# Rescaled tokens from the third group on, and five more pieces by Strassen's scheme, in a two-layer encoder trunk

## Chip, cores and metric

The kernel runs on one core of one Trainium2 chip. Five engines work from their own instruction queues and wait for one another by semaphores: TensorE (PE; its weight loads are listed as PEld), VectorE (DVE), ScalarE (ACT), GpSimd (POOL) and SyncE (SP), which issues the transfers. The metric is the device time of one execution in microseconds, as a median of several runs. The profile comes from one execution.

## What is computed

Two layers over x of shape (1, 512, 1024). Each layer has a token mixer, a cross-attention and an output projection, and then a gated feed-forward part, where the change lies:

```python
def rms_norm(x, g):
    y = xf * lax.rsqrt(jnp.mean(xf * xf, axis=-1, keepdims=True) + EPS)
    return y * g

def conv_ffn(h, w_up, conv_w, conv_b, w_down):
    u = h @ w_up                                   # 1024 -> 2 x 2816
    c = causal depthwise convolution of width 3 of u, + conv_b
    a, g = jnp.split(c, 2, axis=-1)
    return (jax.nn.silu(g) * a) @ w_down           # 2816 -> 1024
...
    h = rms_norm(x, ffn_norm[i])
    x = x + conv_ffn(h, w_up[i], conv_w[i], conv_b[i], w_down[i])
```

The row scale rsqrt(...) is one number per token, the same for all channels. The gain g is one number per channel.

## The kernel before

Activations lie transposed: 128 channels on the partitions, 512 tokens in the free dimension. `xT[k]` (k = 0 to 7) are the eight residual tiles of a layer. Every operand of a matmul is kept as a high and a low part in fp32r (names ending in h or hi, and l or lo); a product is three matmuls, hi x hi, hi x lo and lo x hi (`product`, L401 to L409). Splits are a cast on ScalarE and a subtraction on VectorE: `split_weights` and `combined` for weights (L257, L260, L308, L309, L311, L312), `split` for tokens (L365, L366), `parts_of` for everything else (L1278, L1279).

The feed-forward part (`ffn`) runs over eleven groups q = 0 to 10, in parts of four, four and three (`HALVES`). A group has 256 channels of a (piece `ua`) and 256 of g (piece `ug`). A plain piece is two products, n = 0 and 1, each of eight contraction tiles, 48 matmuls of 128x512 in all. In the text a group's products with the same n, one of a and one of g, are called a step; steps are counted by 2 * q + n. After each product comes `conv`: a multiply by the row scale `rB` on VectorE, in place in PSUM (L1248), then the first tap on ScalarE (L1250) and two taps on VectorE (L1251, L1252). Silu of g is on ScalarE (L1455), the product a * g on VectorE (L1457), and its split (L1278, L1279). The tokens that TensorE reads, `xh` and `xl`, hold x times the gain without the row scale: they are made before `rB` exists. `rB` is computed in `row_scales` behind the first step of group 0.

Pieces listed in `SEVEN` go through `up_by_seven`: Strassen's scheme in Winograd's form, seven products of halves in place of eight. It has 12 matmuls of 128x512 for the first pair of contraction tiles and 63 of 128x256 (L1233) for the other three pairs. It takes four PSUM banks rather than two, sums of weight blocks (`block_sums`, GpSimd, L285), sums of tokens for three pairs (`token_sums`, once per layer) and a decoding of the banks (L1238 to L1244: one copy on ScalarE, six additions on VectorE). `token_sums` scales two tiles by the gain on ScalarE (`scaled`, L1321), combines them by four operations of GpSimd (`combine`, L1286) and splits the results; `SUMS_AT` says behind which step this is done for which pair. The middle sums of a * g for the down projection (`mid_sums`) go through the same `combine`.

After each part comes a down projection (`down`, L1358 for its Strassen products; its decoding and the residual additions are L1375 to L1382). PSUM banks are taken in turn by the eight entries of `TURNS`: mm, mm, sm, sm, lg, lg, tp, tp. Weights come by transfers of 512 KB into three raw buffers, and are split as their six split buffers (`WB`) come free, in program order. The order of the instructions on each engine is settled when the kernel is built: the scheduler interleaves the code above by its dependences; `keep_in_program_order` holds some GpSimd work to the order of the code.

## Time and profile before

| | us |
|---|---|
| median of 3 runs | 1144.44 (1144.1 to 1144.5) |
| profiled execution | 1144.21 |
| its span in the trace | 1142.4 |
| TensorE busy, weight loads busy | 1137.8, 992.9 |
| VectorE, ScalarE, GpSimd busy | 934.7, 619.8, 279.5 |
| groups 0 to 3 of layer 0, first down projection | 241.0 to 328.5, 328.5 to 368.8 |
| groups 4 to 7, second down projection | 368.8 to 454.7, 454.7 to 495.1 |
| groups 8 to 10 | 495.1 to 558.6 |

A row of a timeline reads: start, duration, engine, line, operation, output<-inputs, shapes, and in brackets the idle time before it with what ended it. A row of groups reads: line, engine, operation, names, shapes, count, then busy time and mean ns of one, then the idle time before it and its releasers. Engines pipeline, so the distance from one start to the next is often shorter than the duration: a matmul of 128x512 is listed with 0.39 us and the next starts 0.23 us later.

### The profile page before, as it was taken

Reading aid. Unit: us, or ns where it says so; the run is one execution under the profiler, and the core shown is the slowest. Engines: PE = TensorE matmul, PEld = TensorE weight load, DVE = VectorE, ACT = ScalarE, POOL = GpSimd, SP = SyncE. Lnnn points to the kernel's source line nnn. Section 1 sums busy time; section 2 is a strip of 40 time slices with the busy share of each in tenths; the row PEclk is TensorE's granted clock in tenths of the full one; section 3 lists DMA queues with packets and bytes.
Section 4 is the critical chain, followed back from the end, with each engine's and each line's share of the span. In section 5 each row is a group of like instructions: output and inputs, shape, how many; then the busy total and the mean of one; then the engine's idle time right before and its main releaser. Section 6 shows DMA issues by size and latency. Waiting matters only on the chain.

```text
span 1142.4 us, 17519 instructions
## 1 busy us (share of the span) xinstructions
PE 1137.8 (100%) x6554; PEld 992.9 (87%) x6554; DVE 934.7 (82%) x1553; ACT 619.8 (54%) x1097; POOL 279.5 (24%) x326
## 2 busy tenths in 40 slices
PE   9999999999999999999999999999999999999998
PEld 7888888888899888999888888988888989899888
DVE  7676778689989899999777636778888988999997
ACT  6676687556554355445557634536664434544552
POOL 0000000004364425760000000000246432575240
PEclk9999999999999999999999999999999999999999
DMA  8522242132313332243252330234222243234312
GB/s 290 175 74 96 79 143 70 59 112 78 125 57 129 100 104 74 89 134 112 88 178 72 94 96 19 82 125 140 74 74 93 93 129 93 92 94 130 105 52 102
DMA packets 39666, 117.87 MB, mean 103 GB/s; under 512 B 4767, under 2 KB 7256, under 8 KB 39582
## 3 DMA queue, kind: packets, MB, share of 16 engines
q1 hardware_dynamic: 39150, 116.37, 32.1%
q8 instruction: 51, 0.84, 0.3%
q10 hardware_dynamic: 432, 0.39, 0.1%
q14 instruction: 33, 0.27, 0.1%
HBM read 112.54 MB, written 4.21 MB: 102 GB/s over the span
## 4 chain that ended last, share of the span: by engine, by line
PE 99%; DMA 0%; DVE 0%; issue 0%; SPq 0%; ACT 0%
PE ps_mm L407 6%; PE ps_mm L408 6%; PE ps_mm L409 6%; PE ps_mm L385 6%; PE ps_mm L387 6%; PE ps_mm L386 6%; PE ps_lg L1358 5%; PE ps_sm L407 4%; PE ps_sm L408 4%; PE ps_sm L409 4%; PE ps_mm L1358 4%; PE ps_tp L1358 4%; PE ps_sm L1358 3%; PE ps_tp L224 3%; PE ps_lg L1233 3%; PE ps_tp L408 3%
## 5 line engine op out<-in xcount | busy, mean ns | idle before, releaser
L260 DVE TENSOR_TENSOR wlo<-raw,whi 128x1024 fp32r<-128x1024 f32 (+5 forms) x165 | 185.9, 1139 | 76.4 <-ACT whi L257 74.2
L257 ACT CAST whi<-raw 128x1024 fp32r<-128x1024 f32 (+5 forms) x165 | 157.2, 967 | 101.2 <-PE ps_mm L408 20.3
L285 POOL TENSOR_TENSOR wsum<-raw 128x256 f32<-128x256 f32 (+1 forms) x112 | 99.6, 910 | 115.2 <-DMA raw<-in_wpack_dram 56.5
L385 PE MATMUL ps_mm<-whi,xsh 128*128 128x512 f32 (+2 forms) x328 | 126.4, 385 | 0.0
L387 PE MATMUL ps_mm<-whi,xsl 128*128 128x512 f32 (+2 forms) x328 | 123.1, 375 | 0.0
L386 PE MATMUL ps_mm<-wlo,xsh 128*128 128x512 f32 (+2 forms) x328 | 122.9, 375 | 0.0
L407 PE MATMUL ps_mm<-xsh,whi 128*128 128x512 f32 x294 | 115.6, 393 | 0.0
L408 PE MATMUL ps_mm<-xsl,whi 128*128 128x512 f32 x294 | 114.7, 390 | 0.0
L409 PE MATMUL ps_mm<-xsh,wlo 128*128 128x512 f32 x294 | 114.6, 390 | 0.0
L311 ACT CAST whi<-wsum 128x1024 fp32r<-128x1024 f32 (+1 forms) x56 | 53.6, 957 | 49.3 <-POOL wsum L285 43.7
L1286 POOL TENSOR_TENSOR cvo<-cvo 128x256 f32<-128x256 f32 x56 | 47.4, 866 | 134.3 <-DVE cvo L1457 133.2
L408 PE MATMUL ps_sm<-xsl,whi 128*128 128x512 f32 x202 | 78.7, 389 | 0.0
L407 PE MATMUL ps_sm<-xsh,whi 128*128 128x512 f32 x202 | 78.7, 389 | 0.0
L409 PE MATMUL ps_sm<-xsh,wlo 128*128 128x512 f32 x202 | 78.6, 389 | 0.0
L312 DVE TENSOR_TENSOR wlo<-wsum,whi 128x1024 fp32r<-128x1024 f32 (+1 forms) x56 | 67.1, 1198 | 7.1 <-ACT whi L311 5.6
L385 PEld LDWEIGHTS ps_mm<-whi,xsh 128*128 128x128 f32 x328 | 61.8, 188 | 11.4 <-issue 1.0
L387 PEld LDWEIGHTS ps_mm<-whi,xsl 128*128 128x128 f32 x328 | 61.7, 188 | 11.3
L386 PEld LDWEIGHTS ps_mm<-wlo,xsh 128*128 128x128 f32 x328 | 61.9, 189 | 10.1
L1263 POOL MEMSET xsh<- 128x128 f32 x2 | 0.4, 210 | 276.4 <-PE ps_sm L408 189.9
L409 PEld LDWEIGHTS ps_mm<-xsh,wlo 128*128 128x128 f32 x294 | 55.2, 188 | 11.6
L407 PEld LDWEIGHTS ps_mm<-xsh,whi 128*128 128x128 f32 x294 | 55.3, 188 | 11.3 <-issue 0.3
L408 PEld LDWEIGHTS ps_mm<-xsl,whi 128*128 128x128 f32 x294 | 55.3, 188 | 11.2 <-DVE xsl L366 0.4
(446 smaller groups left out, 3173.7 us busy)
## 6 DMA issues: line engine op xcount, KB each, us to landing
raw<-in_wpack_dram SPq DMA_DIRECT2D x178, 512.0 KB, 3.6
xt<-in_x_t_dram SPq DMA_DIRECT2D x15, 256.0 KB, 5.1
raw<-in_wpack_dram SPq DMA_DIRECT2D x15, 256.0 KB, 2.9
raw<-in_wpack_dram SPq DMA_DIRECT2D x8, 384.0 KB, 3.3
xres<-xt SPq DMA_DIRECT2D x8, 256.0 KB, 3.4
xt<-xres SPq DMA_DIRECT2D x8, 256.0 KB, 5.5
out_dram<-xt SPq DMA_DIRECT2D x7, 256.0 KB, 2.0
bt<-bias_d SPq DMA_DIRECT2D x6, 256.0 KB, 4.0
```

Source lines behind the costliest of these rows:

```text
L257: ins = A.copy(hi[:, c], raw[:, c])
L260: V.tensor_sub(lo[:, c], raw[:, c], hi[:, c].bitcast(F32))
L285: tc.keep_in_program_order(getattr(G, "tensor_" + op)(o, x, y))
L311: A.copy(h1[:, m], wsum[:, m])
L312: V.tensor_sub(l1[:, m], wsum[:, m], h1[:, m].bitcast(F32))
L385: mm(p, sh[k][:, blk(b)], hi, start=k == 0, stop=False)
L386: mm(p, sh[k][:, blk(b)], lo, start=False, stop=False)
L387: mm(p, sl[k][:, blk(b)], hi, start=False, stop=k == KT - 1)
L407: mm(p, hi[:, blk(n)], bh, start=i == first, stop=False)
L408: mm(p, hi[:, blk(n)], bl, start=False, stop=False)
L409: mm(p, lo[:, blk(n)], bh, start=False, stop=i == last)
L1358: mm(banks[c][b][:, h], w, v, start=b not in seen[c], stop=m == nq - 1 and t == 2 and i in close)
```

## The change

From group 2 on the tokens already carry the row scale: `rescale` multiplies `xT[k]` by `rB` on GpSimd, splits the result with the gain, and collects the eight tiles in `fresh`; `FRESH_AT` says behind which step which tiles are made (three behind step 0, three behind step 1, two behind step 2). `conv` leaves the multiply out where the tokens are `fresh`. The token sums are now made of scaled tokens (`scaled` multiplies by gain and `rB` in one instruction of VectorE, before by the gain alone on ScalarE) and stand behind steps 4, 5 and 6 rather than 1, 2 and 3. Their tiles and those of `fresh` swap the buffers that they come from. Five pieces are added to `SEVEN`: `ua` of group 4 and `ug` of group 5 in both layers, `ua` of group 10 in layer 0. In group 5 both pieces then go by Strassen's scheme, one behind the other, and hold all eight banks; before, group 9 of layer 0 alone did so.

```diff
-SEVEN = (('ua', 0, 5), ('ua', 0, 6), ('ua', 0, 8), ('ua', 0, 9), ('ua', 1, 5), ('ua', 1, 6), ('ua', 1, 8), ('ua', 1, 9), ('ug', 0, 9))
-SUMS_AT = {1:(4,5),2:(0,1),3:(2,3)}
+SEVEN = (('ua', 0, 4), ('ua', 0, 5), ('ua', 0, 6), ('ua', 0, 8), ('ua', 0, 9), ('ua', 1, 4), ('ua', 1, 5), ('ua', 1, 6), ('ua', 1, 8), ('ua', 1, 9), ('ug', 0, 5), ('ug', 1, 5), ('ug', 0, 9), ('ua', 0, 10))
+SUMS_AT = {4: (4, 5), 5: (0, 1), 6: (2, 3)}
+FRESH_AT = {0: (0, 1, 2), 1: (3, 4, 5), 2: (6, 7)}
...
+        fresh = []
+
+        def rescale(ks):
+            for k in ks:
+                t = ctile()
+                tc.keep_in_program_order(G.tensor_mul(t, xT[k], rB))
+                hi, lo = split_tiles(pool, "vs", 12) if k < 6 else split_tiles()
+                split(hi, lo, t, c_ffn(l, k))
+                fresh.append((hi, lo))
+
         def conv(p, j):
-            V.tensor_mul(p, p, rB)
+            if tokens is not fresh:
+                V.tensor_mul(p, p, rB)
...
         def scaled(k):
             t = ctile()
-            A.activation(t, xT[k], AF.Copy, scale=c_ffn(l, k))
+            V.scalar_tensor_tensor(t, xT[k], c_ffn(l, k), rB, op0=ALU.mult, op1=ALU.mult)
             return t
...
-            tiles = [split_tiles(pool, "vs", 12) for _ in range(2)]
+            tiles = [split_tiles() for _ in range(2)]
...
+                if q == 2:
+                    tokens = fresh
...
+                    if 2 * q + n in FRESH_AT:
+                        rescale(FRESH_AT[2 * q + n])
                     if 2 * q + n in SUMS_AT:
                         token_sums(SUMS_AT[2 * q + n])
```

GpSimd's queue in the feed-forward part of layer 0, from the first entry behind `row_scales` on. Of before, a token sum (the rows with wsum), the middle sums of group 0, then the next token sums:

```order
L1286 TENSOR_TENSOR wsum<-cvo 128x256
L1286 TENSOR_TENSOR wsum<-cvo,wsum 128x256
L1286 TENSOR_TENSOR wsum<-cvo 128x256
L1286 TENSOR_TENSOR wsum<-cvo,wsum 128x256
L1286 TENSOR_TENSOR cvo<-cvo 128x256 x4
```

Of the change (L1253 is `rescale`, L1298 `combine`, L286 the sums of a weight block):

```order
L1253 TENSOR_TENSOR cvo<-xt,rB 128x512 x6
L1298 TENSOR_TENSOR cvo<-cvo 128x256 x4
L1253 TENSOR_TENSOR cvo<-xt,rB 128x512 x2
L1298 TENSOR_TENSOR cvo<-cvo 128x256 x4
L1298 TENSOR_TENSOR wsum<-cvo 128x256
L1298 TENSOR_TENSOR wsum<-cvo,wsum 128x256
```

The eight multiplies stand around group 0's middle sums, and the first token sum has moved behind group 1's.

VectorE's queue in group 2, from the first product of its step 4 on. Of before:

```order
L1248 TENSOR_TENSOR ps_mm<-ps_mm,rB 128x512
L1457 TENSOR_TENSOR cvo<-cvo 128x512
L1279 TENSOR_TENSOR vsl<-wsum,vsh 128x512
L1279 TENSOR_TENSOR mid<-cvo,mid 128x256
L1251 SCALAR_TENSOR_TENSOR cvo<-ps_mm,cv_81,cvo 128x511
L1252 SCALAR_TENSOR_TENSOR cvo<-ps_mm,cv_81,cvo 128x510
```

Of the change (L1263 and L1264 are the taps of `conv`, L1333 is `scaled`):

```order
L1263 SCALAR_TENSOR_TENSOR cvo<-ps_mm,cv_81,cvo 128x511
L1264 SCALAR_TENSOR_TENSOR cvo<-ps_mm,cv_81,cvo 128x510
L1333 SCALAR_TENSOR_TENSOR cvo<-xt,cols,rB 128x512
L1263 SCALAR_TENSOR_TENSOR cvo<-ps_mm,cv_81,cvo 128x511
L1333 SCALAR_TENSOR_TENSOR cvo<-xt,cols,rB 128x512
L1264 SCALAR_TENSOR_TENSOR cvo<-ps_mm,cv_81,cvo 128x510
L1291 TENSOR_TENSOR mid_3061<-cvo,mid_3060 128x512 x2
```

The multiplies by `rB` are gone, and the scalings of the token sums stand between the taps.

TensorE's queue in group 5 of layer 0, where its g piece starts. Of before (plain, behind the last matmuls of the a piece):

```order
L1233 MATMUL ps_lg<-vsl,whi 128x256
L1233 MATMUL ps_lg<-vsh,wlo 128x256
L407 MATMUL ps_mm<-xsh,whi 128x512
L408 MATMUL ps_mm<-xsl,whi 128x512
L409 MATMUL ps_mm<-xsh,wlo 128x512
```

Of the change, in the same piece, where its first pair of tiles ends and the 256-column products begin:

```order
L408 MATMUL ps_sm<-xsh,whi 128x512
L409 MATMUL ps_sm<-xsl,whi 128x512
L410 MATMUL ps_sm<-xsh,wlo 128x512
L1234 MATMUL ps_sm<-vsh,whi 128x256
L1234 MATMUL ps_sm<-vsl,whi 128x256
L1234 MATMUL ps_sm<-vsh,wlo 128x256
```

The piece has changed from 48 wide matmuls into two banks to 12 wide and 63 narrow ones into four.

## The prediction

> **What bounds the kernel now.** First the page: its busy line, the granted clock, the chain's shares by engine.
>
> ```profile
> span 1142.4 us, 17519 instructions
> PE 1137.8 (100%) x6554; PEld 992.9 (87%) x6554; DVE 934.7 (82%) x1553; ACT 619.8 (54%) x1097; POOL 279.5 (24%) x326
> PEclk9999999999999999999999999999999999999999
> PE 99%; DMA 0%; DVE 0%; issue 0%; SPq 0%; ACT 0%
> ```
>
> TensorE is busy from end to end at full clock, and the chain that ends last is TensorE for 99%. A busy PE could still hide gaps, so next come its waits (for whom; us in total, times, longest).
>
> ```profile
> PE ps_tp L512 <- PEq L1524: 0.8, 1, 0.8
> PE ps_mm L586 <- DVE wlo L260: 0.3, 1, 0.3
> PE ps_mm L586 <- ACT xsh L365: 0.2, 1, 0.2
> ```
>
> All waits are 1.3 us, none in the feed-forward part. So the time is the length of TensorE's own instruction stream; another engine costs something only when it becomes late for TensorE. Removing work from VectorE (82% busy) is worth nothing by itself.
>
> Third, windows cut at the first matmul of each piece: plain, Strassen (sixth group's a), plain behind it (its g), and the ninth group's pair, both Strassen. The window's length is the piece's time.
>
> ```profile
> core 0: us, PE busy (x) PEld busy (x) DVE busy (x) ACT busy (x) POOL busy (x), PEclk, DMA share, GB/s
> 379.74:390.62 10.88, 10.88 (x49) 9.02 (x48) 9.37 (x12) 5.58 (x8) 2.43 (x4) 1.00 0.18 49
> 390.62:400.90 10.28, 10.28 (x77) 9.81 (x75) 7.57 (x9) 4.78 (x8) 5.14 (x6) 1.00 0.49 152
> 400.90:411.80 10.90, 10.90 (x50) 9.02 (x49) 9.14 (x14) 5.06 (x8) 2.79 (x4) 1.00 0.15 51
> 516.26:526.54 10.28, 10.28 (x77) 9.81 (x75) 8.85 (x13) 6.12 (x10) 0.00 (x0) 1.00 0.36 104
> 526.54:536.84 10.30, 10.30 (x78) 9.81 (x77) 10.22 (x15) 5.66 (x8) 0.00 (x0) 1.00 0.36 129
> ```
>
> **The change, part by part. First the five pieces.** By the code a plain piece has 48 matmuls of 512 columns: 10.88 / 48 = 0.227 us each. A Strassen piece has 12 of 512 and 63 of 256: (10.28 - 12 x 0.227) / 63 = 0.120 us each. So 36 of 512 go (8.16 us) and 63 of 256 come (7.56): 0.60 us saved; about 0.02 is given back where a plain piece follows (10.90 for 10.88). The side-by-side pair, here 10.28 and 10.30, behaves like two single ones. Five pieces at 0.58 us: **-2.9 us**, bounds 2.8 and 3.0. The order of TensorE's instructions has 135 = 5 x 27 rows more, so all five are really converted; SyncE's has as many as before, so no transfers are added.
>
> The Trainium skill has a rule that speaks against this sum. Its page "TensorE: Matmul & The Clock Gate", section "Back-to-back issue gap", gives a sustained spacing of about 131 ns at 512 columns and 81 ns at 128; a straight line between them would put 256 columns at 98 ns (estimate). By that the pieces would lose 63 x 0.098 - 36 x 0.131 = 1.5 us each, 7.3 us in all. The trace does not agree: 0.227 and 0.120 us, measured on this kernel's operands.
>
> **The row scale.** From the third group on the product is already scaled, so VectorE's multiply by rB (L1248), four per group in nine groups a layer, goes: 36 x 0.69 = 24.8 us. VectorE gains per layer eight low halves of the rescaled tokens (like L366) and six scalings that ScalarE had (L1321): 14 x 0.75 = 10.5 us. Each new piece adds six decoding adds and more weight splits.
>
> ```profile
> L1248 DVE TENSOR_TENSOR ps_sm<-ps_sm,rB 128x512 f32<-128x512 f32 x28 | 19.3, 691 | 1.7 <-PE ps_sm L409 1.7
> L366 DVE SCALAR_TENSOR_TENSOR xsl<-xt,cols,xsh 128x512 fp32r<-128x512 f32 x16 | 12.0, 747 | 0.8 <-ACT xsh L365 0.8
> L1239 DVE TENSOR_TENSOR cvo<-cvo,ps_tp 128x256 f32<-128x256 f32 x4 | 1.7, 421 | 2.1 <-ACT cvo L1238 2.1
> L260 DVE TENSOR_TENSOR wlo<-raw,whi 128x1024 fp32r<-128x1024 f32 x125 | 153.0, 1237 | 67.3 <-ACT whi L257 65.4 <-PE ps_lg L790 1.3
> L260 DVE TENSOR_TENSOR wlo<-raw,whi 128x896 fp32r<-128x896 f32 x9 | 11.4, 1265 | 1.7 <-ACT whi L257 1.5
> L312 DVE TENSOR_TENSOR wlo<-wsum,whi 128x512 fp32r<-128x512 f32 x12 | 10.7, 890 | 3.1 <-PE ps_lg L1233 1.6 <-ACT whi L311 1.5
> L309 DVE TENSOR_TENSOR wlo<-raw,whi 128x768 fp32r<-128x768 f32 x44 | 49.7, 1130 | 0.6 <-ACT whi L308 0.6
> L312 DVE TENSOR_TENSOR wlo<-wsum,whi 128x1024 fp32r<-128x1024 f32 x44 | 56.4, 1282 | 4.0 <-ACT whi L311 4.0
> ```
>
> A new piece: decoding 4 x 0.42 + 2 x 0.69 = 3.1 us, splits 1.27 + 0.89 + 1.13 + 1.28 = 4.57 in place of 2 x 1.24, so +2.1: together 5.2 us of VectorE. Over a whole layer VectorE gets lighter, by 24.8 - 10.5 less two or three times 5.2. That is no gain in time, since nobody waits for it; it only pays for the pieces: in the sixth group, side by side, 16.7 busy us of the two windows above - 4 x 0.69 + 5.2 = 19.1 of 20.6, so it fits. GpSimd makes eight weight sums more per piece, some 7 us at 0.9, and has 5.14 + 2.79 there. All of this costs 0 while both stay ahead.
>
> It does not get lighter at once. Groups three and four also inherit the token sums (six low halves) that stood three pieces earlier.
>
> ```profile
> 285.00:328.52 43.52, 43.52 (x193) 36.06 (x192) 39.81 (x49) 22.87 (x34) 21.00 (x25) 1.00 0.29 93
> ```
>
> Of the 39.8 us, 8 x 0.69 = 5.5 go; 6 x 0.75 = 4.5 (scalings), about 2.5 more token-sum halves at 0.96 = 2.4 (row below) and one token half of 0.75 come: 42.0 of 43.5 us, 1.5 to spare where it had 3.7. I take this as no delay: part of the old 3.7 was waiting, between the rB multiply and the ScalarE step that needed it, and this hop is gone there. Below nothing it can't bring time either, as TensorE has no wait there.
>
> ```profile
> L1279 DVE TENSOR_TENSOR vsl<-wsum,vsh 128x512 fp32r<-128x512 f32 x12 | 11.5, 962 | 4.2 <-ACT vsh L1278 4.2
> L1286 POOL TENSOR_TENSOR cvo<-cvo 128x256 f32<-128x256 f32 x56 | 47.4, 866 | 134.3 <-DVE cvo L1457 133.2
> L285 POOL TENSOR_TENSOR wsum<-raw,wsum 128x256 f32<-128x256 f32 x44 | 49.5, 1124 | 3.5
> ```
>
> **GpSimd's eight multiplies** of 128x512 have no row. The nearest are 256-column ones: 0.87 us (the same cost, if a start-up dominates) up to 2 x 1.12 = 2.25; I take 1.8, twice 0.9, since its duration follows width in the nearest rows. Six come before the first mid sums, two behind them, queued on GpSimd where the token sums were. They cost nothing if the tokens are ready when the third group starts. The last one is the test.
>
> ```profile
> 284.55 0.39 PE L408 MATMUL ps_tp<-xsl,whi 128*128 128x512 f32 x1
> 289.99 0.39 PE L408 MATMUL ps_mm<-xsl,whi 128*128 128x512 f32 x1
> L257 ACT CAST whi<-raw 128x1024 fp32r<-128x1024 f32 x125 | 129.5, 1051 | 76.4 <-DMA raw<-in_wpack_dram 17.4 <-PE ps_mm L408 12.4 <-PE ps_sm L408 12.0
> L365 ACT ACTIVATE xsh<-xt,cols 128x512 fp32r<-128x512 f32 x16 | 11.5, 717 | 3.9 <-DVE xt L1131 3.9
> 273.88 3.41 POOL L1286 TENSOR_TENSOR cvo<-cvo 128x256 f32<-128x256 f32 x4 [1.99 <-DVE cvo L1457]
> ```
>
> GpSimd: mid sums until 277.3, then two multiplies, 281. On ScalarE the eighth token's cast stands behind a weight cast that waits for the second-last matmul at 284.55, done about 284.8: 284.8 + 1.05 + 0.72 = 286.6, its low half on VectorE 287.3. TensorE needs it at 289.99: 2.7 us to spare. Behind that cast on ScalarE stand the second group's last convolution step and silu, whose banks nobody needs before the fourth group. GpSimd itself has 4 us before it enters that chain.
>
> **Sum:** 1144.21 - 2.9 = 1141.3 for the profiled execution (span 1142.4 - 2.9 = 1139.5, and the 1.8 us around it). The median of before lies 0.23 higher, so the median after is **1141.5 us**. What a measurement of this kernel can tell from no change is about 0.2%, 2.3 us; the forecast lies only 0.6 beyond it.
>
> **Rivals. (1) VectorE late in the first down projection.** This one ends slower. TensorE's tightest place is there, in both layers:
>
> ```profile
> 356.75 1.21 DVE L312 TENSOR_TENSOR wlo<-wsum,whi 128x1024 fp32r<-128x1024 f32 x1
> 359.36 0.28 PE L1358 MATMUL ps_lg<-mid,wlo 128*128 128x256 f32 x1
> 905.76 1.21 DVE L312 TENSOR_TENSOR wlo<-wsum,whi 128x1024 fp32r<-128x1024 f32 x1
> 908.24 0.28 PE L1358 MATMUL ps_lg<-mid,wlo 128*128 128x256 f32 x1
> ```
>
> The low weights end 1.40 us (359.36 - 357.96) and 1.27 us before their matmul. If VectorE comes d later out of the fourth group, TensorE loses (d - 1.40) + (d - 1.27). It is faster than the bound only for d under 1.6 and slower than before by the bound for d over 3.9. What could make d: 42.0 - 39.8 = 2.2 us if none of the idle time is used, and a slower VectorE beside GpSimd:
>
> ```profile
> 284.88 1.22 DVE L1279 TENSOR_TENSOR vsl<-wsum,vsh 128x512 fp32r<-128x512 f32 x1
> 287.16 0.68 DVE L1279 TENSOR_TENSOR vsl<-wsum,vsh 128x512 fp32r<-128x512 f32 x1
> 284.37 1.18 POOL L1286 TENSOR_TENSOR wsum<-cvo,wsum 128x256 f32<-128x256 f32 x1
> ```
>
> The same operation takes 1.22 beside a running GpSimd sum and 0.68 without. By the order of GpSimd two token sums more, eight operations at 0.87, fall into these 43.5 us: 7 us, 16% of the time. About half of VectorE's 49 instructions there read two tiles of SBUF; 0.16 x 25 x 0.54 = 2.2. Together d = 4.4: 2 x 4.4 - 2.67 = 6.1 us lost, **1147.6**. With half of it, d = 2.2, 1.7 are lost: 1143.2. For it: the tight 42.0. Against it: the idle time that goes with the hop.
>
> The same point is a rule of the Trainium skill: "GPSIMD Engine Reference", section "Key points", says GpSimd shares its SBUF interfaces with VectorE and contends with VectorE's instructions that have two SBUF inputs. It speaks against the change, which gives both engines more of just these; by it rival 1, without it the forecast. The trace agrees: 1.22 beside 0.68 us.
>
> **(2) The rescaled tokens come late.** The weight cast ahead of the eighth token needs its transfer, whose buffer is freed by a split behind the mid sums' halves.
>
> ```profile
> raw<-in_wpack_dram SPq DMA_DIRECT2D x178, 512.0 KB, 3.6
> ```
>
> Mid sums done at 277.3, their casts and halves and that split about 280.2, landed 283.8: before the matmul that the cast waits for. With the four sums at 1.8 each (7.1 for 3.41) it lands at 287.5, and 1.05 + 0.72 + 0.75 later, 290.0, the token is ready: 0 to 0.3 us a layer. From there each microsecond counts once per layer: 1 us gives 1141.5 + 2 x 1.2 = **1143.9**.
>
> **(3) Side by side fills all eight banks.** The seventh group's first piece needs banks that the sixth's decoding and convolution must have left.
>
> ```profile
> 534.18 0.74 DVE L1252 SCALAR_TENSOR_TENSOR cvo<-ps_sm,cv,cvo 128x510 f32<-128x510 f32 x1
> 536.84 0.40 PE L407 MATMUL ps_sm<-xsh,whi 128*128 128x512 f32 x1
> ```
>
> In the ninth group this is met with 1.9 us (536.84 - 534.92). The new places are lighter (no rB multiply, 1.4 us a pair), but have GpSimd's sums ahead of the weights. Late by 2 us in each layer: 4 less the 1.9 already free, 1143.6 at most; I expect 0.
>
> **(4) It doesn't do what it says**: weight loads pace the narrow matmuls. In a Strassen window the loads take 9.81 / 75 = 0.131 us each; at that pace a piece has 63 x 0.131 + 12 x 0.227 = 11.0 us, 0.1 over the plain one: 1144.44 + 0.5 = **1144.9**. The windows show the loads overlapped, 10.28 us for the piece, so this would have to come only with the new places. By the Trainium skill's spacing quoted above the change would even end at 1144.44 + 7.3 = 1151.7; the rows speak against it, and its chance is inside this rival's.
>
> **Chances.** Forecast 0.57; rival 1 0.25 (half of it within the bound, half slower); rival 2 0.07 and rival 3 0.07, both mostly within; rival 4 0.04. So faster by over 0.2% 0.57, within 0.26, slower 0.17. The range goes from 3.0 saved and the half microsecond of waits that could go, 1141.0, to **1147.0**, which takes in rivals 2 to 4 and the larger part of rival 1; its last part above that is under 0.15.
>
> **What would show it.** Right: TensorE's windows of the fifth group's and sixth group's first and second pieces at 10.28 to 10.30 in both layers, the eleventh's first piece too, TensorE's waits at 1.3 us, and a span near 1139.5. Wrong by rival 1: a wait of ps_lg, ps_mm or ps_tp at the down projection's matmuls (L1358 before) for wlo; by rival 2, a wait of ps_mm for xsl where the third group starts; by rival 3, a wait for VectorE's last convolution step. If a wait shows where I have none of these, a weight or token sum of GpSimd is late, and the chain there will name it.

## The result, and the profile after

The changed kernel takes **1156.55 us** (median of four runs, 1156.29 to 1157.15) against 1144.43 (four runs, 1144.1 to 1144.5): 1.0107 times as long, with an interval of 1.009 to 1.0125, or 12.1 us slower. The forecast was 1141.5 with a range up to 1147.0; the time lies far outside. The profiled execution took 1157.15 us, its span is 13.0 longer than before. Groups are counted from one below, as in the prediction: the sixth is group 5 of the code.

The page's head, with the chain's shares by engine:

```profile
span 1155.4 us, 17931 instructions
PE 1141.2 (99%) x6689; PEld 999.7 (87%) x6689; DVE 942.3 (82%) x1549; ACT 625.9 (54%) x1116; POOL 353.4 (31%) x382
PE 75%; DVE 17%; POOL 3%; issue 2%; ACT 2%; DMA 1%; DVEq 0%; ACTq 0%; POOLq 0%
```

VectorE's share of the span is what it was, 82%, and TensorE still reads 99% (100% before). Only the chain tells that something has turned: it was TensorE for 99%, and now runs for a quarter through VectorE, GpSimd and what they are issued. TensorE's waits in the feed-forward parts name the places:

```profile
PE ps_lg L1370 <- ACT whi L312: 3.3, 2, 1.8
PE ps_lg L1370 <- DVE wlo L313: 2.5, 4, 0.9
PE ps_sm L408 <- DVE cvo L1264: 2.2, 2, 1.1
PE ps_sm L1370 <- DVE mid L1291: 1.3, 2, 1.1
PE ps_tp L408 <- DVE cvo L1264: 0.6, 2, 0.4
PE ps_mm L409 <- DVE xsl L367: 0.3, 1, 0.3
```

L1370 is the down projection's narrow matmul (L1358 before), L408 a wide one of the up projections. A wait is counted from the modelled end of the matmul ahead, so the distance from start to start grows by up to 0.28 us more. That distance gives the whole account (us, from TensorE's first matmul of a stretch to that of the next):

| stretch | before | after | difference |
|---|---|---|---|
| layer 0, third and fourth groups | 43.52 | 44.33 | +0.81 |
| layer 0, first down projection | 40.32 | 46.03 | +5.71 |
| layer 0, fifth to eighth groups | 85.90 | 86.49 | +0.59 |
| layer 0, ninth to eleventh groups | 63.56 | 62.99 | -0.57 |
| layer 1, first down projection | 40.32 | 45.83 | +5.51 |
| layer 1, fifth to eighth groups | 85.90 | 86.66 | +0.76 |

They add to 12.81; what stands ahead of the third group is 0.23 later, and all other stretches are as long as before, within 0.05 in all. So the table accounts for the 13.0 us between the spans. The pieces and the stretches of layer 0 as windows of after; the first two rows are the third and fourth groups and the first down projection, then the fifth group's a, the sixth's a and g, the seventh's a and the eleventh's a:

```profile
core 0: us, PE busy (x) PEld busy (x) DVE busy (x) ACT busy (x) POOL busy (x), PEclk, DMA share, GB/s
285.23:329.56 44.33, 44.05 (x193) 35.88 (x192) 41.70 (x50) 21.32 (x32) 26.57 (x27) 1.00 0.28 84
329.56:375.59 46.03, 42.83 (x337) 42.01 (x336) 43.03 (x55) 21.64 (x31) 33.14 (x34) 0.96 0.26 83
375.59:385.89 10.30, 10.30 (x77) 9.81 (x76) 8.65 (x13) 3.60 (x6) 4.99 (x5) 1.00 0.58 177
396.80:407.07 10.27, 10.27 (x76) 9.80 (x75) 8.18 (x12) 5.73 (x10) 2.65 (x3) 1.00 0.19 53
407.07:417.73 10.66, 10.46 (x78) 9.80 (x76) 8.70 (x13) 4.32 (x7) 7.85 (x10) 1.00 0.30 98
417.73:429.33 11.60, 10.51 (x76) 9.86 (x76) 11.38 (x17) 6.67 (x10) 0.00 (x0) 1.00 0.48 138
544.17:554.47 10.30, 10.30 (x78) 9.81 (x76) 10.06 (x15) 6.70 (x11) 0.00 (x0) 1.00 0.41 136
```

The converted pieces are as short as forecast: 10.30 for the fifth and eleventh groups' a, and 10.66 for the sixth's g, of which 0.36 is a wait at its end. So five pieces did bring their 2.9 us. In the fifth to eighth groups they hide part of the loss: 0.59 and 0.76 are two pieces (-1.16) and 1.75 and 1.92 lost at waits. By far the largest part, 11.2 us, was lost in the two first down projections.

What happens there is read best from GpSimd's own row of work. Before, the sums of the down projection's first and second weight block start one behind the other (the first two rows; a block's sums are L285 before and L286 after). The third row is the next block:

```profile
318.69 1.44 POOL L285 TENSOR_TENSOR wsum<-raw 128x256 f32<-128x256 f32 x2
321.60 2.36 POOL L285 TENSOR_TENSOR wsum<-raw 128x256 f32<-128x256 f32 x2
328.87 2.16 POOL L285 TENSOR_TENSOR wsum<-raw 128x256 f32<-128x256 f32 x2 [2.36 <-DVE wlo L312]
```

After, the four sums of the third token sum (L1298) stand between them:

```profile
322.53 1.88 POOL L286 TENSOR_TENSOR wsum<-raw 128x256 f32<-128x256 f32 x2
...
326.67 0.74 POOL L1298 TENSOR_TENSOR wsum<-cvo 128x256 f32<-128x256 f32 x1
...
329.86 1.18 POOL L1298 TENSOR_TENSOR wsum<-cvo,wsum 128x256 f32<-128x256 f32 x1
333.67 2.38 POOL L286 TENSOR_TENSOR wsum<-raw 128x256 f32<-128x256 f32 x2 [2.63 <-DVE wlo L313]
```

The second block starts 12.1 us later than before. GpSimd works for only 4.4 us of them on the token sum; 3.8 us are there before the first block begins, 1.2 are the first block's own sums, which took longer, and the last 2.63 are the brackets' wait. Weight and token sums share two buffers in turn (both are called wsum). The token sum took the second, and the second block must wait until VectorE has split the first, at 333.6. Before, the second block found a buffer free, and it was the third that waited for this split, until 328.8.

So the split itself is 4.8 us later too, though GpSimd had finished the first block at 326.7: ScalarE's cast of it and the split stand behind VectorE's earlier work. In this stretch VectorE had no idle time even before the change, and it has none after (a window of before, then one of after):

```profile
320.10:334.20 14.10, 14.10 (x86) 12.62 (x86) 14.03 (x16) 7.05 (x10) 11.51 (x13) 1.00 0.27 76
319.50:337.50 18.00, 18.00 (x112) 16.18 (x110) 17.96 (x20) 8.88 (x14) 15.11 (x15) 1.00 0.08 30
```

Ahead of the split its queue now has two low halves of the second token sum (1.22 and 1.27 us) and two scalings of the third (2.41). From the second block the lateness goes to TensorE, by ScalarE's cast and VectorE's low half:

```profile
338.31 1.05 ACT L312 CAST whi<-wsum 128x1024 fp32r<-128x1024 f32 x1 [3.82 <-POOL wsum L286]
339.39 1.34 DVE L313 TENSOR_TENSOR wlo<-wsum,whi 128x1024 fp32r<-128x1024 f32 x1 [1.86 <-ACT whi L312]
339.41 0.50 PE L1370 MATMUL ps_lg<-mid,whi 128*128 128x256 f32 x2 [1.77 <-ACT whi L312]
340.78 0.39 PE L1370 MATMUL ps_lg<-mid,wlo 128*128 128x256 f32 x1 [0.87 <-DVE wlo L313]
341.42 0.75 DVE L1264 SCALAR_TENSOR_TENSOR cvo<-ps_tp,cv,cvo 128x510 f32<-128x510 f32 x1
```

VectorE idles 1.86 us for the cast at the head of its own queue. Behind it stand the fourth group's last convolution tap (341.42; before it started at 333.51), the product of a and g, and the split of its middle sums, so TensorE waits for mid as well later on.

### The profile page after: what moved, and what is told of

Its sections match the earlier page's. It is cut to its first block, busy times and chain, and to the rows that moved or that the text cites. A ratio compares the mean times of both kernels' runs of the same rounds, so it can differ in the third digit from the quotient of the medians.

```text
span 1155.4 us, 17931 instructions
## 1 busy us (share of the span) xinstructions
PE 1141.2 (99%) x6689; PEld 999.7 (87%) x6689; DVE 942.3 (82%) x1549; ACT 625.9 (54%) x1116; POOL 353.4 (31%) x382
## 4 chain that ended last, share of the span: by engine, by line
PE 75%; DVE 17%; POOL 3%; issue 2%; ACT 2%; DMA 1%; DVEq 0%; ACTq 0%; POOLq 0%
PE ps_mm L386 6%; PE ps_mm L388 6%; PE ps_mm L387 6%; PE ps_lg L1370 3%; PE ps_mm L409 3%; PE ps_mm L408 3%; PE ps_mm L410 3%; PE ps_sm L408 3%; PE ps_sm L410 3%; PE ps_sm L409 3%; PE ps_mm L1370 3%; PE ps_tp L225 3%; PE ps_tp L1370 3%; PE ps_lg L408 2%; PE ps_lg L410 2%; PE ps_lg L409 2%
## 5 line engine op out<-in xcount | busy, mean ns | idle before, releaser
L286 POOL TENSOR_TENSOR wsum<-raw 128x256 f32<-128x256 f32 (+1 forms) x132 | 115.3, 894 | 95.3 <-DVE wlo L313 38.8
L1298 POOL TENSOR_TENSOR cvo<-cvo 128x256 f32<-128x256 f32 x56 | 57.9, 1053 | 133.7 <-DVE cvo L1471 132.6
L1290 ACT CAST mid<-cvo 128x512 fp32r<-128x512 f32 x82 | 46.6, 578 | 43.0 <-DVE cvo L1471 36.3
L286 POOL TENSOR_TENSOR wsum<-wsum,raw 128x256 f32<-128x256 f32 (+1 forms) x66 | 67.2, 1019 | 0.0
L1291 DVE TENSOR_TENSOR mid<-cvo,mid 128x512 fp32r<-128x512 f32 x82 | 60.9, 762 | 6.2 <-ACT mid L1290 6.0
L286 POOL TENSOR_TENSOR wsum<-raw,wsum 128x256 f32<-128x256 f32 (+1 forms) x66 | 62.8, 952 | 5.2
L1469 ACT ACTIVATE cvo<-cvo 128x512 f32<-128x512 f32 x44 | 27.8, 632 | 63.8 <-DVE cvo L1264 63.7
L310 DVE TENSOR_TENSOR wlo<-raw,whi 128x768 fp32r<-128x768 f32 (+1 forms) x52 | 56.7, 1090 | 3.1 <-ACT whi L309 2.8
L1370 PE MATMUL ps_mm<-mid,whi 128*128 128x256 f32 x304 | 58.6, 283 | 0.0
L1370 PE MATMUL ps_lg<-mid,whi 128*128 128x256 f32 x280 | 55.0, 286 | 3.3 <-ACT whi L312 3.3
L408 PE MATMUL ps_mm<-xsh,whi 128*128 128x512 f32 x142 | 56.5, 398 | 0.0
```

Of the source, the lines that this page charges most:

```text
L286: tc.keep_in_program_order(getattr(G, "tensor_" + op)(o, x, y))
L408: mm(p, hi[:, blk(n)], bh, start=i == first, stop=False)
L1370: mm(banks[c][b][:, h], w, v, start=b not in seen[c], stop=m == nq - 1 and t == 2 and i in close)
```

## The experiments

The first theory after the trace: the third token sum, moved behind step 6, holds up the down projection's second weight block on GpSimd and its two buffers (theory Q, the queue). The rival is rival 1 of the prediction as it was written: VectorE has too much to do in the third and fourth groups (theory V). A third, P, puts the loss on the pieces. Times below are medians beside runs of the kernel before on the same chip (1144.0 to 1144.2).

The texts put ahead of the runs were written before them and use other names. Runs e1 to e8 are experiments 1 to 8, e11 is 9, e12 is 10, e18 is 11; e9, e10, e13 and e15 are 12 to 15, e17 is 16, e16 is 17 and e19 is 18. Theory 1a is V, 1b is Q, and theory 1 leaves open which of the two. Their groups are counted from 0.

**1. The row scale and the moved sums, without new pieces.** After with the list of pieces of before:

```diff
-SEVEN = (('ua', 0, 4), ... ('ug', 0, 5), ('ug', 1, 5), ('ug', 0, 9), ('ua', 0, 10))
+SEVEN = (('ua', 0, 5), ('ua', 0, 6), ... ('ua', 1, 9), ('ug', 0, 9))
```

> The row scale and the moved token sums alone, with the nine Strassen pieces of before. Theory 1 (VectorE and GpSimd are overfilled in groups 2 and 3 by rescaled tokens and token sums, and the first down projection waits): the losses at the first down projection stay, 5.7 us in layer 0 and 5.5 in layer 1 by the trace of the change, and the 0.7 at the start of group 2; the losses at group 6 go. 1144.4 + 11.9 = about 1156. Rival (the weight sums of the new piece in group 4, which GpSimd makes beside the first down projection, are what is late): no loss there, 1144 to 1145.

1156.42 us, 1.0107 (1.0087 to 1.0127): +12.3. All of the first down projection's loss is there without a new piece (45.98 and 45.78 us long), with the waits for whi, wlo and mid of after; the waits in the seventh group are not. P falls for the first down projection.

**2. The new pieces without the row scale.** Before with the list of after:

```diff
-SEVEN = (('ua', 0, 5), ('ua', 0, 6), ... ('ua', 1, 9), ('ug', 0, 9))
+SEVEN = (('ua', 0, 4), ... ('ug', 0, 5), ('ug', 1, 5), ('ug', 0, 9), ('ua', 0, 10))
```

> The five new pieces without the row scale: the tokens and the token sums as before. Theory 1: no wait in the first down projection; the pieces give 2.9 us; the side-by-side pair of group 5, with the rB multiplies still there, costs at least what it costs in the change (1.8 us a layer, waits at the first matmuls of group 6), so 1144.4 - 2.9 + 3.7 or more, 1145 to 1149. Rival (the first down projection waits because of the new piece of group 4): 1144.4 - 2.9 + 11 + 3.7 = about 1156.

1162.08 us, 1.0157 (1.0136 to 1.0177): +18.0, far above what I expected. The first down projection is untouched (40.31). TensorE's waits:

```profile
PE ps_sm L407 <- DVE cvo L1252: 4.7, 2, 2.5
PE ps_sm L1358 <- ACT mid L1278: 4.2, 2, 2.1
PE ps_tp L407 <- DVE cvo L1252: 1.6, 2, 0.9
```

The first and the third row are the seventh group, as in after but more than twice as long. The second is new: the cast of middle sums that the second down projection waits for (45.65 and 45.19 us long instead of 40.3). I had priced only the first kind. With the row scale the side by side piece costs less: the two halves of the change are +12.3 and +18.0 alone and +12.1 together.

**3. Three kinds of pieces on before.** The fifth group's a in both layers and the eleventh's a, no pieces side by side:

```diff
+SEVEN = (('ua', 0, 4), ('ua', 0, 5), ... ('ua', 1, 4), ... ('ug', 0, 9), ('ua', 0, 10))
```

> Before with only three of the five pieces (a of group 4 in both layers, a of group 10 in layer 0), nothing side by side in group 5, no row scale. Theory 1: nothing waits, 1144.4 - 3 x 0.58 = 1142.7. Rival (VectorE needs the saved multiplies for the extra pieces): a wait of 1 us or more behind group 4's piece, 1144 or more.

1149.48 us, 1.0045 (1.0028 to 1.0061), where I expected a gain. The largest wait is at the end of layer 0's feed-forward part, for a bank:

```profile
PE ps_mm L385 <- DVE xt L1131: 2.1, 1, 2.1
PE ps_mm L1358 <- DVE mid L1279: 1.4, 3, 0.7
```

A Strassen piece takes four banks and a plain one two, so each converted piece shifts the turn of the eight banks for all that follows; here the next part asks first for the bank that is read last. Experiment 9 has one new piece in layer 0 and after has three, and neither has such a wait. With the granted clock at 0.50 behind it (window 594.6 to 598.0) it costs 3.9 us from start to start. The other waits stand in the second down projections, 41.55 and 41.87 us long instead of 40.31: VectorE is late there, as the rival of the expectation had it.

**4. The change without its side by side pieces.** `('ug', 0, 5), ('ug', 1, 5)` taken out of the list of after.

> The change without the two pieces that go side by side in group 5. If the losses at group 6 (1.8 and 1.9 us) come from the four banks held by each piece and VectorE being late there, they go, and 2 x 0.58 of savings with them: 1156.5 - 3.7 + 1.2 = 1154.0. Rival (they are the lateness of groups 2 and 3 carried on): the waits at group 6 stay and the time is 1157.7.

1158.21 us, 1.0123 (1.0103 to 1.0143): slower than after. The time alone would speak for the rival; the trace does not. The waits of the seventh group are gone, which is worth 2.5 us net of the two pieces. A wait at the end of layer 0, for the turn of the banks as in experiment 3, costs 3.8, again with the granted clock at 0.50 behind it (598.5 to 601.9):

```profile
PE ps_mm L386 <- DVE xt L1132: 2.1, 1, 2.1
```

Experiments 5 to 8 and 12 to 16 start from the kernel of experiment 1, so that the first down projection stands alone.

**5. The scaling of the token sums back on ScalarE** (the sums then lack rB):

```diff
-            V.scalar_tensor_tensor(t, xT[k], c_ffn(l, k), rB, op0=ALU.mult, op1=ALU.mult)
+            A.activation(t, xT[k], AF.Copy, scale=c_ffn(l, k))
```

> The row scale alone as in e1, with the six scalings of the token sums back on ScalarE; they then lack rB, so the token sums are made of tokens without the row scale. VectorE loses six operations that took 0.96 us each in e1 in groups 2 and 3, 5.7 us; GpSimd's queue keeps all its work in the same order. Theory 1a (VectorE's backlog is what comes late): VectorE enters the down projection some 5 us earlier and the 11 us lost there fall to 3 or less, 1144.4 + 0.7 + 3 = 1148 or less. Theory 1b (GpSimd's queue is the bound: the third token sum stands between the weight sums, which share its two sum buffers): the wait for whi stays, 1154 to 1156.

1150.42 us, 1.0053 (1.0032 to 1.0073): half of the loss goes with six VectorE instructions a layer. That speaks for V as a part of the cause. But the second weight block is still late (330.7), and 6.3 us stay. TensorE no longer waits for that block; VectorE does, and TensorE then waits for the fourth group's middle sums, which stand behind it (the wait for mid is 1.1 us in each layer):

```profile
335.96 1.36 DVE L313 TENSOR_TENSOR wlo<-wsum,whi 128x1024 fp32r<-128x1024 f32 x1 [2.57 <-ACT whi L312]
PE ps_sm L1370 <- DVE mid L1291: 2.2, 2, 1.1
```

**6. The third token sum two steps later**, behind the down projection (it then takes tokens to which that projection has added):

```diff
-SUMS_AT = {4: (4, 5), 5: (0, 1), 6: (2, 3)}
+SUMS_AT = {4: (4, 5), 5: (0, 1), 8: (2, 3)}
```

> The row scale alone as in e1, with the third token sum moved from step 6 behind step 8, that is behind the first down projection; it then reads the residual after that projection, so these sums are of other tokens. Theory 1b (the third token sum in GpSimd's queue between the weight sums): the first wait of the down projection (1.9 and 1.7 us for whi) goes wholly, and nearly all of the loss, 1145 to 1147. Theory 1a (VectorE's backlog over all of groups 2 and 3): VectorE is relieved by a third of the 13 us that the sums cost it there, so about half of the loss stays, 1149 to 1151.

1146.12 us, 1.0018 (1.0007 to 1.0028): +2.0 remain of 12.3. VectorE still does the first two sums and the rescaled tokens; V alone was expected to leave about half. But the third sum's work on VectorE is moved too, so this run does not part Q from V. GpSimd's first two weight blocks now follow each other:

```profile
321.85 1.88 POOL L286 TENSOR_TENSOR wsum<-raw 128x256 f32<-128x256 f32 x2
325.69 2.33 POOL L286 TENSOR_TENSOR wsum<-raw 128x256 f32<-128x256 f32 x2
```

**7. All token sums two steps earlier**, made from the rescaled tokens:

```diff
-SUMS_AT = {4: (4, 5), 5: (0, 1), 6: (2, 3)}
+SUMS_AT = {2: (4, 5), 3: (0, 1), 4: (2, 3)}
-            (bh, bl), (fh, fl) = (tokens[k] for k in ks)
+            (bh, bl), (fh, fl) = (fresh[k] for k in ks)
```

> The row scale alone as in e1, with the token sums two steps earlier (behind steps 2, 3 and 4 rather than 4, 5 and 6), made of the rescaled tokens that are there by then. Nothing is left out. Theory 1a: the work is the same and VectorE is full from the start of group 1 on, so the backlog is carried on, less the idle time of about 2 us a layer that is left earlier: 1151 to 1155. Theory 1b: the weight sums of the down projection find the sum buffers free, the waits for whi and wlo go: 1145 to 1147. Against both, the tokens at the start of group 2 could be later than in e1 (0.7 us there).

1159.47 us, 1.0131 (1.0115 to 1.0148), a miss for both theories. The sums collide with the rescaling: TensorE now waits 1.9 us in all for rescaled tokens and up to 2.1 at once for low halves of weights. It shows how full the place is, but does not tell Q from V.

**8. One GpSimd operation of four in each token sum**, the rest replaced by a copy on ScalarE:

```diff
-            combine(scaled(ks[0]), scaled(ks[1]), G, [sum_tile()], parts)
+            b2, b1, s = scaled(ks[0]), scaled(ks[1]), sum_tile()
+            tc.keep_in_program_order(G.tensor_sub(s[:, :S], b1, b2))
+            A.copy(s[:, S:], b2)
+            parts([s])
```

> The row scale alone as in e1, with each token sum's four GpSimd operations replaced by one GpSimd operation of 128x512 and a copy on ScalarE; the sums are then not the ones needed. VectorE has the same instructions. GpSimd has some 1.5 to 2 us per sum less, and VectorE's operations are slowed less beside it. Theory 1b: the first wait shrinks by about 2 us, the loss per layer by 3: 1150 to 1151. Theory 1a: VectorE gains only what the slowing costs it, 2 us at most: the loss per layer falls by 1 to 2, 1152 to 1154.

1153.39 us, 1.0078 (1.0058 to 1.0099). The one operation that is left is twice as wide and takes 1.29 us where the four took 4.4. That is worth 3 us of 12, and the second block still starts at 332.3, after 4.70 us of idle time that end with VectorE's split of the first. So GpSimd's work is not what holds it alone; Q in that simple form falls, and the buffer, VectorE or both hold it too.

**9. The eleventh group's a alone, on before.** `('ua', 0, 10)` added to the list of before.

> Before with one new piece only, a of group 10 in layer 0, no row scale. The four-bank piece moves the turn of the banks by two, as the three pieces of layer 0 in e3 did by four: there the last bank of layer 0's down projection was then mm, which the next layer's first product takes, and waited 2.1 us. Here the last is tp. If that wait was the turn of the banks: no wait at the layer's end, 1144.2 - 0.6 = 1143.6. If it was VectorE being late behind the extra piece: the wait stays, 1145 or more.

1143.66 us (ten runs), 0.9995 (0.9985 to 1.0004): -0.5, where a piece is worth 0.58, and not told apart from no change. The one wait left, 0.8 us at L512, is one that before has too.

**10. The seventh group's wait.** After, with the fifth group's middle sums (group 4 of the code) replaced by copies on ScalarE:

```diff
-            q = combine(*c2, E, [ctile(), ctile()], parts)
+            if skip:
+                x = [ctile(), ctile()]
+                A.copy(x[0], c2[0])
+                A.copy(x[1], c2[1])
+                parts(x)
...
-                    mids.append(mid_sums(c2, ops, V if end else G))
+                    mids.append(mid_sums(c2, ops, V if end else G, q == 4))
```

> The change, with the four GpSimd operations of group 4's middle sums replaced by two copies on ScalarE (the sums are then not the ones needed). In the trace of the change they took 4.7 us, 404.3 to 409.0, ahead of the weight sums that VectorE waited for at 412.4 before it could decode group 5's a piece. If GpSimd's queue is what makes the bank late: the waits at the first matmuls of group 6 (1.8 and 1.9 us a layer) go or fall under 0.5, 1156.5 - 3.5 = 1153. If VectorE's own work is: they stay within 0.5 us, 1155.5 to 1156.5.

1153.31 us, 1.0079 (1.0059 to 1.0099), 3 less than after, as expected. The waits for VectorE's last tap are gone, those of the first down projection stay:

```profile
PE ps_lg L1377 <- ACT whi L312: 3.4, 2, 1.8
PE ps_lg L1377 <- DVE wlo L313: 2.5, 4, 0.9
PE ps_sm L1377 <- DVE mid L1291: 2.2, 2, 1.1
```

So these waits begin with GpSimd's middle sums; whether by its queue alone or also by slowing VectorE beside them, the run doesn't part. In after, the sixth group's weight sums queue behind those middle sums, and VectorE's decoding and taps behind the low half of these weights:

```profile
404.34 4.72 POOL L1298 TENSOR_TENSOR cvo<-cvo 128x256 f32<-128x256 f32 x4 [9.26 <-DVE cvo L1471]
...
412.41 1.25 DVE L313 TENSOR_TENSOR wlo<-wsum,whi 128x512 fp32r<-128x512 f32 x1 [1.55 <-ACT whi L312]
...
416.84 1.40 DVE L1264 SCALAR_TENSOR_TENSOR cvo<-ps_tp,cv,cvo 128x510 f32<-128x510 f32 x2
417.73 0.47 PE L408 MATMUL ps_tp<-xsh,whi 128*128 128x512 f32 x1 [0.20 <-DVE cvo L1264]
...
429.33 0.47 PE L408 MATMUL ps_sm<-vsh,whi 128*128 128x512 f32 x1 [1.09 <-DVE cvo L1264]
```

**11. A second place side by side.** The ninth group's g (group 8 of the code) added to before, where GpSimd makes no middle sums:

```diff
-SEVEN = (... ('ug', 0, 9))
+SEVEN = (... ('ug', 0, 9), ('ug', 0, 8))
```

> Before with the g piece of group 8 in layer 0 by Strassen's scheme too, so that groups 8 and 9 of layer 0 each have their pair side by side; no row scale. In these groups GpSimd makes no middle sums (its windows of the ninth group are empty). If the loss behind group 5's pair was GpSimd's queue: at most 0.5 us of wait at the first matmuls of group 9, 1144.1 - 0.6 = 1143.5 to 1144. If it was the eight banks with VectorE behind: the waits come here too, 2 to 4 us as in e2, 1146 to 1149. VectorE's window of the ninth group was 10.2 of 10.3 us full before, which speaks for some lateness in any case.

1146.25 us, 1.0022 (1.0012 to 1.0031): slower, though GpSimd's last sum there ended at 521.1, long before the wait. It stands at 539.0, at the start of the eleventh group and behind both pairs, and is for a bank that VectorE's last tap frees; VectorE was busy for 10.3 of 10.3 us in each of the two pieces ahead. So eight full banks can come late from VectorE's queue, with GpSimd idle:

```profile
PE ps_lg L407 <- DVE cvo L1252: 1.8, 1, 1.8
```

**12 to 14. The three ties of the third token sum, cut one at a time.** First its VectorE work (scalings left out, low halves as copies of ScalarE):

```diff
-                    parts_of(t[0][:, blk(i, S)], hi, lo)
-            combine(scaled(ks[0]), scaled(ks[1]), G, [sum_tile()], parts)
+                    if ks[0] == 2:
+                        A.copy(hi, t[0][:, blk(i, S)])
+                        A.copy(lo, t[0][:, blk(i, S)])
+                    else:
+                        parts_of(t[0][:, blk(i, S)], hi, lo)
+            ins = (xT[k] if ks[0] == 2 else scaled(k) for k in ks)
+            combine(*ins, G, [sum_tile()], parts)
```

> The row scale alone as in e1, in which the third token sum (step 6) keeps its four GpSimd operations and its place, but has no work on VectorE: it reads the tokens without scaling, and its low parts are copies by ScalarE. These sums are not the ones needed. VectorE is relieved as in e6 (four operations, 4.1 us by the means in e1), GpSimd not. If VectorE's volume is the cause, the time is as in e6, 1146 to 1147; if GpSimd's four operations between the weight sums are, it is near e1, 1153 to 1156.

1153.84 us, 1.0083 (1.0063 to 1.0104): 9.6 of 12.3 stay. Then its GpSimd work:

```diff
+            if ks[0] == 2:
+                x, y, s = scaled(ks[0]), scaled(ks[1]), sum_tile()
+                A.copy(s[:, :S], x)
+                A.copy(s[:, S:], y)
+                parts([s])
+            else:
+                combine(scaled(ks[0]), scaled(ks[1]), G, [sum_tile()], parts)
```

> The row scale alone as in e1, in which the third token sum keeps its VectorE work and its place, but the four GpSimd operations are replaced by two copies on ScalarE; the sums are not the ones needed. GpSimd is relieved as in e6, VectorE only of the slowing beside GpSimd. If VectorE's volume is the cause: 1152 to 1155, with the waits for mid and wlo still there. If GpSimd's queue is: 1146 to 1148.

1153.0 us, 1.0076 (1.0056 to 1.0096): 8.8 stay. Then the shared buffer: all token sums go into the convolution's own tiles.

```diff
-                    parts_of(t[0][:, blk(i, S)], hi, lo)
-            combine(scaled(ks[0]), scaled(ks[1]), G, [sum_tile()], parts)
+                    parts_of(t[i], hi, lo)
+            combine(scaled(ks[0]), scaled(ks[1]), G, [ctile(), ctile()], parts)
```

> The row scale alone as in e1, with the token sums written to two tiles of the convolution's buffers each, not to the two sum buffers that the weight sums use. Work, order and results are as in e1. If the shared buffer is the cause: the second weight sum of the down projection starts when GpSimd has finished the third token sum, about 331.0 rather than 333.6, 2.6 us earlier, and the waits for whi and wlo go: about half of the loss, 1149 to 1151. If it is the work of VectorE and GpSimd: no change, 1155.5 to 1156.5.

1155.03 us, 1.0095 (1.0075 to 1.0115): the wait for the buffer is gone, and GpSimd's order takes its place, with nearly the same start of the second block:

```profile
326.96 4.98 POOL L1298 TENSOR_TENSOR cvo<-cvo 128x256 f32<-128x256 f32 x4
331.91 2.87 POOL L286 TENSOR_TENSOR wsum<-raw 128x256 f32<-128x256 f32 x2
```

**15. Two ties cut, the buffer kept**: GpSimd's and VectorE's work on the third sum both replaced by copies on ScalarE (the edits of 12 and 13 together).

> The row scale alone as in e1, with the third token sum's place and sum buffer kept and filled and read by ScalarE copies only; neither VectorE nor GpSimd works for it (the sums are not the ones needed). If the shared buffer is the cause: still 1151 to 1153, since the second weight sum waits for the first one's split. If the joint work is: as e6, 1146 to 1147.

1150.73 us, 1.0058 (1.0038 to 1.0078). GpSimd now stands idle for 5.23 us ahead of the second block, with no work of its own left there; what the bracket names is ScalarE's copy out of the shared buffer:

```profile
330.68 1.44 POOL L286 TENSOR_TENSOR wsum<-raw 128x256 f32<-128x256 f32 x2 [5.23 <-ACT xsl L1344]
```

**16. The third sum one step later**, behind step 7 instead of 6, the last place from which it still gets the tokens that it needs:

```diff
-SUMS_AT = {4: (4, 5), 5: (0, 1), 6: (2, 3)}
+SUMS_AT = {4: (4, 5), 5: (0, 1), 7: (2, 3)}
```

> The row scale alone as in e1, with the third token sum behind step 7 rather than 6; nothing is left out. In GpSimd's queue it then stands behind three weight sums of the down projection instead of behind one. If the place between the weight sums is the cause: the waits for whi at 339 go, and VectorE's work moves 10 us later, into the down projection, where the waits for wlo at 360 and for mid stay or grow by 1 to 2 us a layer: 1147 to 1150. If VectorE's volume is: nothing is won, 1154 to 1157.

1164.17 us, 1.0176 (1.0161 to 1.0191), a miss. The second block is early (326.0), but on VectorE, which has no idle time from 319.2 to 350, the sum's scalings and low halves now stand ahead of and between the fourth group's middle sums, and these come late. This is theory V's kind of loss, at another place:

```profile
PE ps_sm L1370 <- ACT mid L1290: 8.3, 2, 4.1
PE ps_sm L1370 <- DVE mid L1291: 4.2, 4, 1.8
```

**17 and 18. More pieces on before.** The eleventh group's a in both layers (`('ua', 0, 10), ('ua', 1, 10)`):

> Before with a of group 10 by Strassen's scheme in both layers. e11 (layer 0 alone) had no wait and 1143.7. In layer 1 the down projection behind it has the smallest slack of the trace of before, 0.9 us, and the piece adds 5 us of VectorE's work in front of it. If VectorE has room: 1143.1. If not: a wait of 1 us or more there, 1144 to 1146.

1155.42 us, 1.0101 (1.0084 to 1.0118), far above both expectations: in the last down projection of layer 1 TensorE waits once 4.7 and once 2.3 us for a last tap. And the ninth group's g with the eleventh's a, the turn of the banks started two further on in layer 0:

```diff
-SEVEN = (... ('ug', 0, 9))
+SEVEN = (... ('ug', 0, 9), ('ug', 0, 8), ('ua', 0, 10))
-        tokens, sums_of, nb = list(zip(xh, xl)), {}, [0]
+        tokens, sums_of, nb = list(zip(xh, xl)), {}, [2 if l == 0 else 0]
```

> Before with the g piece of group 8 and the a piece of group 10 in layer 0, no row scale, and the turn of the banks in layer 0 started two places on, so that the last bank of the layer is sm and not mm. If VectorE holds in groups 8 to 10: 1144.1 - 1.2 = 1142.9. If it is overfilled there (10 us more work in 63.6 us, of which 6 were idle): it ends some 4 us late and the down projection or the layer's end waits, 1146 to 1149.

1148.15 us, 1.004 (1.0025 to 1.0054): two waits for last taps, up to 2.5 us. No version here beats both kernels by more than can be measured; experiment 9 comes nearest.

Together, for the first down projection (start of the second weight block, length of the down projection in both layers, time over before):

| kernel | second block | length, layer 0 and 1 | over before |
|---|---|---|---|
| before | 321.6 | 40.32, 40.32 | 0 |
| 6: third sum away from there | 325.7 | 40.99, 40.79 | +2.0 |
| 5: scaling on ScalarE | 330.7 | 43.04, 43.07 | +6.3 |
| 15: without GpSimd's and VectorE's work | 330.7 | 43.47, 43.26 | +6.6 |
| 13: without GpSimd's work | 331.3 | 44.57, 44.37 | +8.8 |
| 14: without the buffer | 331.9 | 45.71, 44.89 | +10.9 |
| 8: 1.3 of GpSimd's 4.4 us of work | 332.3 | 44.60, 44.28 | +9.2 |
| 12: without VectorE's work | 332.5 | 44.82, 44.67 | +9.6 |
| 1: row scale and moved sums | 333.6 | 45.98, 45.78 | +12.3 |

The later the second block, the longer the projection; 14 alone falls out of the order. (16 and 7 stand apart: they move the wait to other work.) No cut of one tie or of two brings the block ahead of 330.7; only moving the whole sum away does. That the third sum at its place, with all its work, causes 10.3 of the 12.3 us is shown by 6 against 1. How these divide between buffer, GpSimd and VectorE stays open: they cover each other, and in 8, 12, 13 and 15 ScalarE, which casts the same weights, has copies to make in their stead, so each of these may show less than its tie is worth. Of the +2.0 that 6 leaves, its trace puts 1.2 us in the two first down projections and 0.7 ahead of the first, where the rescaled tokens come.

## Why the prediction was wrong

- **The pieces: right.** 0.58 us each, measured 10.27 to 10.30 a piece. The 131 and 81 ns spacing of the Trainium skill ("TensorE: Matmul & The Clock Gate", "Back-to-back issue gap") would have made them longer than plain ones, by the prediction's estimate; the trace disagrees again.
- **"I take this as no delay": the step that failed.** It put VectorE's work in the third and fourth groups at 42.0 of 43.5 us (measured 41.70 of 44.33) and took the 1.5 us left as room to spare. The sum of the work was about right; the room was not where it was needed. VectorE's idle time in after lies almost wholly in four waits for ScalarE, 2.5 us together, all before 319.6. Behind that it had none (17.96 of 18.00 us busy), and had none before the change either (14.03 of 14.10), so the token sums' work there went straight into lateness: the split of the down projection's first weight block ended 4.8 us later. The six scalings also took 0.98 us each on average where 0.75 was counted.
- **"All of this costs 0 while both stay ahead": the condition that wasn't looked at.** GpSimd's share went from 24 to 31%, which looks harmless. But in its queue the third token sum, which fed nothing urgent, had come to stand ahead of the second weight block, and it took the buffer that this block needs. So the block waited for the late split and began 12.1 us late; 11.2 us were lost in the two first down projections. The order of the queue was there to be read before: which entries the sum is moved ahead of, and which buffer it takes. The prediction worked that through for the eight multiplies, and not for the third sum.
- **Rival 1 had the place and a part of the mechanism, not the size.** It named the down projection, the wait for wlo and ps_lg, and a VectorE that comes 4.4 us late; the first split was 4.8 late. It had the loss at 6.1 us, and 11.2 were lost, because it did not have the second block behind the sum. Experiment 12 takes the third sum's work off VectorE and leaves 9.6; experiment 5 takes the scalings of all three off and leaves 6.3.
- **Rival 3: "I expect 0", measured 3.7.** (1.75 + 1.92.) Its price of "2 us in each layer" was right. The reason against it, lighter VectorE, was met in the pair's two windows (16.9 us busy, 19.1 forecast); the one for it that I had written beside, GpSimd's sums ahead of the weights, decided. Experiments 10 and 11 show two ways to the same wait.
- **Rival 2: came, small, in layer 0 only.** The last rescaled token was worked out for 287.3 and was done at 290.8; VectorE began its low half at 290.09 instead of 286.6:

```profile
290.09 0.75 DVE L367 SCALAR_TENSOR_TENSOR xsl<-cvo,cols,xsh 128x512 fp32r<-128x512 f32 x1
290.90 0.50 PE L409 MATMUL ps_mm<-xsl,whi 128*128 128x512 f32 x1 [0.28 <-DVE xsl L367]
```

- **GpSimd's multiply: near what was taken.** 1.8 us was taken, with bounds 0.87 and 2.25; the sixteen took 1.56 us on average, 1.29 at the fastest and 2.29 at the slowest. What late tokens cost is at most the 0.81 us of layer 0's third and fourth groups.
- **Rival 4: no.** The windows stay at 10.3.

## What to carry to other kernels

When work moves to or along a helper engine, write down what stands behind it in that engine's queue, which buffers it takes in turn, and who waits for those: here a sum of 4.4 us, beside a VectorE without idle time at that place, put weights 12 us late while GpSimd was 31% busy. Look for an engine's spare time where the new work falls; an average over two groups hid that there was none. Cutting one of several ties that hold the same instruction shows little; that the step is the cause is shown by taking all of it away. And a piece that takes more banks shifts the turn of all later ones, so pieces can't be added one by one on paper: of the parts alone, one costs 12.3 and the other 18.0 us, both together 12.1.

## What the runs showed of the hardware that was not expected

A short wait can halve TensorE's clock for some microseconds, and need not. In layer 0 of after, behind waits of 1.77 and 0.87 us, the granted clock is 0.53 for 3.6 us; in experiment 10 the same place has the same waits (1.79 and 0.87) and full clock behind them, as has layer 1 of after behind 1.57 and 0.87. The windows right behind the waits, first of after, then of experiment 10:

```profile
341.00:344.60 3.60, 3.60 (x19) 3.60 (x19) 2.77 (x4) 1.85 (x4) 3.52 (x5) 0.53 0.04 15
```

```profile
341.50:345.00 3.50, 3.42 (x29) 3.25 (x28) 2.71 (x4) 2.62 (x4) 3.42 (x5) 1.00 0.00 0
```

19 matmuls against 29 in about the same time. It cost little net: the down projection took 46.03 us with it and 46.05 without, as the slower matmuls waited 0.20 instead of 1.10 us for mid at 348. Experiment 11 has it too, 0.54 from 539.0 to 542.4, behind its wait of 1.8 us; in three of its ten runs, the profiled one among them, the mean granted clock is 0.999, in the other seven 1.000. The Trainium skill ("TensorE: Matmul & The Clock Gate", "What's actually happening") gives one idle window of about 3.4 us, free-running, as what throttles. The lengths of the slow stretches agree with that window; a wait of 1.8 us, half of it, was enough here in some runs, and no run shows what decides it.
